# A convolution's LayerNorm, dealt out over the projections beside it: four chunks added on VectorE and one mean product instead of four

## The chip, the core and the metric

The kernel runs on one core of a Trainium2 chip. It is written by hand for the five engines of the core: TensorE (PE, matrix products, with the loading of its weights shown as PEld), VectorE (DVE), ScalarE (ACT), GpSimd (POOL) and SyncE (SP, which here issues the DMAs). The metric is the device time of one execution in microseconds (us). A tile is an area of on-chip memory with 128 partitions; a product of TensorE lands in one of eight PSUM banks.

## The reference, cut to what matters

Two layers of an encoder are computed for 1024 prompt tokens and 32 sample tokens, with a model width of 1024. The change touches layer 0, the convolution branch. Shortened:

```python
h = einsum('btd,de->bte', x, w_in)                     # all projections of the layer
a_val, a_glu, a_gate, q, k, v, b_gate, f_logit = split(h)
a = a_val * sigmoid(a_glu)                             # 512 channels
a, conv_state = causal_dwconv(a, past_conv, conv_w, conv_b)   # 31 taps for each channel
a = silu(layer_norm(a, cln_g, cln_b)) * silu(a_gate)   # LayerNorm over the 512 channels
...                                                    # q, k, v: attention with forgetting, gated by silu(b_gate)
y = einsum('bte,ed->btd', concatenate([a, o]), w_out)
x = layer_norm(ALPHA * x + y, ln_g, ln_b)
```

The channels lie on the partitions, so the 512 channels are four chunks of 128, and the mean over channels is a sum over partitions and chunks. The kernel makes it with TensorE: a 128x128 matrix that holds 1/512 everywhere (`mean_w`) times a chunk gives the chunk's share of the mean, on all partitions at once.

## The kernel before, in words

Layer 0 begins with a run of projections on TensorE. The input x is held transposed and as two parts, a rounded one and its remainder (x0h, x0l), and so is each weight (whi, wlo), so that one projection of 128 columns is, for each of four token groups (256, 256, 256 and 288 tokens), 24 products into one PSUM bank: whi·x0h, wlo·x0h, whi·x0l, eight each. `proj_steps` (L194 to L216) makes them; after each eight products it calls `tick`, which counts down the work put off with `defer(n, fn)` and runs what is due. A weight comes as one DMA of 512 KB (`wraw`, L114), which ScalarE rounds to whi (L107) and VectorE turns into wlo (L108).

Order of the projections: the values and gates of the convolution (eight projections, with v between), then `a_gate` (four, L852 to L859), then `b_gate` (four, L860 and L861), then for each of four head pairs k and q (`qk0`). A group's result leaves its bank by a ScalarE instruction (L857, L320, L810). For k and q ScalarE writes further copies (L267, L268, L280 to L283), and VectorE remainders.

The depthwise convolution is on VectorE alone: for each chunk one multiplication (L868) and 30 multiply-adds over 1086 tokens (L870). It reads the padded inputs (`apad0` to `apad3`) and writes `acc`. After it comes the LayerNorm (L871 to L887), by four token groups (`g`): four products of `mean_w` with the chunks of acc add up to the mean in a bank (L875); VectorE subtracts it from each chunk (L879), ScalarE squares (L881), four more products give the variance (L882), ScalarE takes the root (L883), VectorE the reciprocal (L884) and scales each chunk (L887). Then ScalarE's Silu (L893), the product with `sga` (L896), a split in two parts (L107, L108) and two DMAs to scratch memory (L898, L899). Both loops stand under `tc.high_priority()`: the scheduler, which sets a fixed order for each engine when the kernel is built, puts them as early as it thinks that their inputs are there. Each engine then runs its own list in order.

Which banks a use may take is set by a table of roles: "j" projections, "s" sums and scores, "t" transposes, "o" outputs. BULK gives j six banks (0 to 5), BULK1 three (0 to 2), ATT two (0 and 1), with s on 2 and 3. Before, BULK holds until after the last `b_gate` projection, and ATT from there on, for the first k and q too.

After the first k and q (`stacks = steps(qk0(0))`) the memory of the convolution is released and attention begins: GpSimd makes a bias from `ckb` (a DMA of 512 KB, L916), TensorE the scores (L288, L289), and k and q of the next head pair are mixed in between.

Of the kernel before, what the change touches and what calls it, by code (L numbers as in the profile page):

```python
# [10 lines left out]
FT = mybir.dt.float32  # L11
# [21 lines left out]
def tile_encoder(ctx: ExitStack, tc, A, O):  # L33
# [25 lines left out]
    def ps_s():  # L59
        return bank("s")  # L60
# [127 lines left out]
    def proj_cm(*args):  # L188
        for _ in proj_steps(*args):
            pass  # L190
# [66 lines left out]
    def rows_out(pl, src_cols, n, dst):  # L257
        ps = ps_t()
        for c in range(4):
            pe.transpose(ps[:n, c * 128:(c + 1) * 128], src_cols(c), ident)  # L260
        st = pl.tile([32, 512], FT, name="rst", tag="rst", bufs=1)
        act.activation(st[:n], ps[:n], AF.Copy)
        sp.dma_start(dst, st[:n])
# [53 lines left out]
    def sgate_evac(l, p, pl):  # L317
        def f(g, t0, n, ps):
            sg = pl.tile([128, 288], FT, name="sgc", tag="sgc", bufs=4 - l)
            act.activation(sg[:, :n], ps, AF.Silu)  # L320
            sp.dma_start(sgd[4 * l + g][:, p, :], sg[:, :256])
            if n > 256:
                sp.dma_start(sgS[l][:, p, :], sg[:, 256:288])
        return f
# [19 lines left out]
    def steps(gen):  # L344

        while True:
            try:
                next(gen)
            except StopIteration as stop:
                return stop.value  # L350
# [330 lines left out]
    with tc.tile_pool(name="p1", bufs=1, reuse_waits="tile") as p1:  # L681
# [35 lines left out]
        for c in range(4):  # L717
            pe.transpose(pcc[:, c * 30:(c + 1) * 30], cc[:, c * 128:(c + 1) * 128], ident[:30, :30])
        apad = []
        for c in range(4):  # L720
            ap_ = p1r.tile([128, 1116], FT, name=f"apad{c}")
            pool.memset(ap_[:, 0:30], 0.0)
            act.activation(ap_[:, 1054:1084], pcc[:, c * 30:(c + 1) * 30], AF.Copy)
            apad.append(ap_)
# [127 lines left out]
    for c in range(4):  # L852
        if c == 0:
            defer(60, forget_sums)

        def ev_ag(g, t0, n, ps, c=c):
            act.activation(sga[:, c, t0:t0 + n], ps, AF.Silu)  # L857
        proj_cm(w0, 1024 + c * 128, 128, X0, ev_ag)
    for p in range(4):  # L859
        proj_cm(w0, 3072 + p * 128, 128, X0, sgate_evac(0, p, p1r))  # L860


    rows_out(p1r, lambda c: apad[c][:, 1024:1054], 30, O["conv_p"])
    rows_out(p1r, lambda c: apad[c][:, 1086:1116], 30, O["conv_s"])
    acc = p1r.tile([128, 4, 1086], FT, name="acc")
    for c in range(4):
        ac = acc[:, c]
        dve.tensor_scalar(ac, apad[c][:, 0:1086], vT[:, c, 0:1], vT[:, c, 31:32], op0=OP.mult, op1=OP.add)  # L868
        for j in range(1, 31):
            dve.scalar_tensor_tensor(ac, apad[c][:, j:j + 1086], vT[:, c, j:j + 1], ac, op0=OP.mult, op1=OP.add)  # L870
    with tc.high_priority():  # L871
        for g, (s0, n) in enumerate(((0, 256), (256, 256), (512, 256), (768, 318))):
            pm = ps_s()[:, :n]
            for c in range(4):
                pe.matmul(pm, mean_w, acc[:, c, s0:s0 + n], start=c == 0, stop=c == 3)  # L875
            pvv = ps_s()[:, :n]
            rstd = p1r.tile([128, 318], FT, name="rstd", tag="rstd", bufs=2)
            for c in range(4):
                dve.tensor_tensor(acc[:, c, s0:s0 + n], acc[:, c, s0:s0 + n], pm, op=OP.subtract)  # L879
                sq = p1r.tile([128, 318], FT, name="sq", tag="sq", bufs=2)  # L880
                act.activation(sq[:, :n], acc[:, c, s0:s0 + n], AF.Square)  # L881
                pe.matmul(pvv, mean_w, sq[:, :n], start=c == 0, stop=c == 3)  # L882
            act.activation(rstd[:, :n], pvv, AF.Sqrt, bias=epst)  # L883
            dve.reciprocal(rstd[:, :n], rstd[:, :n])  # L884
            for c in range(4):
                av = acc[:, c, s0:s0 + n]
                dve.tensor_tensor(av, av, rstd[:, :n], op=OP.mult)  # L887
    with tc.high_priority():
        sgh, acl = sga.bitcast(FR), acc.bitcast(FR)
        for g, (s0, n) in enumerate(((0, 256), (256, 256), (512, 256), (768, 318))):  # L890
            for c in range(4):
                av = acc[:, c, s0:s0 + n]
                act.activation(av, av, AF.Silu, bias=vT[:, c, 33:34], scale=vT[:, c, 32:33])  # L893
            for a0, b0, m, dst in ((s0, s0, 256, cad[0][g]), (1054, SEQ, DS, caS[0]))[:1 + g // 3]:
                av = acc[:, :, a0:a0 + m]
                dve.tensor_tensor(av, av, sga[:, :, b0:b0 + m], op=OP.mult)  # L896
                split(sgh[:, :, b0:b0 + m], acl[:, :, a0:a0 + m], av)
                sp.dma_start(dst[0], sga[:, :, b0:b0 + m])  # L898
                sp.dma_start(dst[1], av)  # L899

    got0, got1 = {}, {}

# [4 lines left out]
    def resid1(t, rows, r, c0):  # L907
        sp.dma_start(r[:rows, c0:], x1d[t][:rows, c0:c0 + r.shape[1] - c0])

    roles.update(ATT)  # L910
    stacks = steps(qk0(0))
    cctx.close()
    with tc.tile_pool(name="p2", bufs=1, reuse_waits="tile") as p2:
        def fox_bias(h):
# [694 lines left out]
```

## Time and profile before

| what | value |
| --- | --- |
| median of 3 runs | 1265.44 us (1259.82 to 1269.61) |
| the profiled execution | 1263.32 us, its span 1261.3 us (2.0 us lie around it) |
| PE busy | 1195.5 us, 95% of the span |
| VectorE busy | 984.0 us, 78% |
| ScalarE busy | 709.4 us, 56% |
| mean granted clock of TensorE | 0.990 of full speed |

A busy PE in this profile is one whose pipeline holds a product, so the busy share alone doesn't tell how fast work goes through. The start times of successive rows do: what a group of products costs in the queue is the start of the next group less its own start. The stretch that matters lies between about 216 us (the convolution's last multiply-adds) and about 307 us (the first work of attention).

### The profile page before, as it was taken

The page shows a single profiled execution, that of the slowest core. Times are in us where ns is not written, and L with a number is a line of the kernel's source. Part 1 is how long each engine was busy: PE and PEld are TensorE (multiplying, and loading weights), DVE is VectorE, ACT ScalarE, POOL GpSimd, SP SyncE. Part 2 cuts the span into 40 slices and gives each one's busy share as a digit, 9 for nine tenths or more (in the row PEclk, how much of TensorE's full clock was granted, in tenths as well). Part 3 has the DMA queues.
Part 4 walks back from the last instruction along what each step waited for, and adds up shares of the span by engine and source line. Part 5 has one row for each costly group of instructions (what it writes and reads, how often), then busy time and mean ns, then how long its engine had stood idle before and what let it go on. Part 6 is the DMA issues. An engine that isn't in the chain of part 4 may idle for free.

```text
span 1261.3 us, 25216 instructions
## 1 busy us (share of the span) xinstructions
PE 1195.5 (95%) x9351; PEld 1133.3 (90%) x9353; DVE 984.0 (78%) x2061; ACT 709.4 (56%) x1525; POOL 263.9 (21%) x590
## 2 busy tenths in 40 slices
PE   8999999998998988999999999999899999889997
PEld 7999999998888987999987999999888888869997
DVE  5699999367877778648948979999688878896376
ACT  5111241379787887322257789787577877874110
POOL 0000034002433333000111257666211111100000
PEclk9999999999999999999999999999999999899899
DMA  7113422236332274533252232323333223624412
GB/s 225 51 35 94 124 59 63 80 117 181 86 92 85 68 235 153 186 114 118 84 133 61 82 99 58 93 69 82 82 83 88 61 76 96 203 91 163 122 39 100
DMA packets 163302, 130.29 MB, mean 103 GB/s; under 512 B 35850, under 2 KB 151010, under 8 KB 163180
## 3 DMA queue, kind: packets, MB, share of 16 engines
q1 hardware_dynamic: 163180, 128.69, 34.5%
q8 instruction: 73, 1.20, 0.4%
q14 instruction: 49, 0.40, 0.1%
HBM read 82.93 MB, written 40.31 MB: 98 GB/s over the span
## 4 chain that ended last, share of the span: by engine, by line
PE 66%; DVE 13%; ACT 11%; issue 4%; DMA 3%; SPq 1%; POOL 1%; DVEq 0%; ACTq 0%; POOLq 0%
PE bank L207 31%; PE bank L571 14%; PE bank L240 4%; PE bank L419 3%; PE bank L394 3%; ACT s L373 2%; PE bank L288 2%; PE bank L289 2%; DVE ptl L108 2%; DVE wt L1088 1%; ACT pth L107 1%; DMA rps<-rpx 1%; DVE s L370 1%; PE bank L223 1%; PE bank L252 1%
## 5 line engine op out<-in xcount | busy, mean ns | idle before, releaser
L870 DVE SCALAR_TENSOR_TENSOR acc<-apad,vT,acc 128x1086 f32<-128x1086 f32 x120 | 156.2, 1340 | 1.1
L108 DVE TENSOR_TENSOR ptl<-bank,pth 128x512 fp32r<-128x512 f32 (+1 forms) x160 | 99.3, 633 | 39.2 <-ACT pth L107 37.9
L207 PE MATMUL bank<-x1h,whi 128*128 128x256 f32 (+3 forms) x848 | 125.9, 286 | 0.1
L207 PE MATMUL bank<-x1l,whi 128*128 128x256 f32 (+3 forms) x848 | 124.9, 287 | 0.0
L207 PE MATMUL bank<-x1h,wlo 128*128 128x256 f32 (+3 forms) x848 | 123.8, 286 | 0.0
L207 PE MATMUL bank<-x0h,whi 128*128 128x256 f32 (+1 forms) x768 | 113.7, 288 | 1.5 <-ACT kr L810 1.0
L207 PEld LDWEIGHTS bank<-x1h,whi 128*128 128x128 f32 (+1 forms) x848 | 111.8, 187 | 2.1 <-ACT rpx L979 0.5
L207 PEld LDWEIGHTS bank<-x1h,wlo 128*128 128x128 f32 (+1 forms) x848 | 112.3, 187 | 1.5
L419 PE MATMUL bank<-ident,s 128*128 128x128 f32 x576 | 96.7, 281 | 17.8 <-DVE ptl L108 11.4
L207 PEld LDWEIGHTS bank<-x1l,whi 128*128 128x128 f32 (+1 forms) x848 | 111.9, 188 | 0.9
L207 PE MATMUL bank<-x0h,wlo 128*128 128x256 f32 (+1 forms) x768 | 111.7, 286 | 0.0
L373 ACT ACTIVATE s<-s,mn 128x896 f32<-128x896 f32 (+7 forms) x128 | 98.8, 773 | 22.3 <-DVE mn L370 21.2
L207 PE MATMUL bank<-x0l,whi 128*128 128x256 f32 (+1 forms) x768 | 110.4, 284 | 0.0
L107 ACT ACTIVATE pth<-bank 128x512 fp32r<-128x512 f32 (+1 forms) x160 | 85.8, 549 | 35.8 <-PE bank L419 33.8
L108 DVE TENSOR_TENSOR wlo<-wraw,whi 128x1024 fp32r<-128x1024 f32 (+2 forms) x62 | 75.3, 1215 | 39.2 <-ACT whi L107 39.1
L207 PEld LDWEIGHTS bank<-x0h,whi 128*128 128x128 f32 x768 | 101.4, 190 | 3.7 <-ACT kr L810 1.3
L1112 ACT ACTIVATE jka<-sc,neg 128x768 bf16<-128x768 f32 (+2 forms) x96 | 99.6, 1037 | 4.3 <-POOL neg L1139 1.7
L207 PEld LDWEIGHTS bank<-x0h,wlo 128*128 128x128 f32 x768 | 100.8, 189 | 0.8
L207 PEld LDWEIGHTS bank<-x0l,whi 128*128 128x128 f32 x768 | 100.0, 188 | 0.7
L107 ACT ACTIVATE whi<-wraw 128x1024 fp32r<-128x1024 f32 (+2 forms) x62 | 65.0, 1049 | 57.0 <-PE bank L207 35.5
L419 PEld LDWEIGHTS bank<-ident,s 128*128 128x128 f32 x576 | 67.0, 142 | 32.9 <-DVE ptl L108 11.3
L394 PE MATMUL bank<-pth,v 128*128 128x256 f32 x320 | 92.6, 308 | 3.0 <-ACT pth L107 2.6
(422 smaller groups left out, 2705.0 us busy)
## 6 DMA issues: line engine op xcount, KB each, us to landing
wraw<-in_o_w_in_dram SPq DMA_DIRECT2D x26, 512.0 KB, 4.1
wraw<-in_e_w_in_dram SPq DMA_DIRECT2D x24, 512.0 KB, 4.1
sgd<-sgc SPq DMA_DIRECT2D x32, 128.0 KB, 3.0
out_dram<-ko SPq DMA_DIRECT2D x16, 256.0 KB, 2.3
vf<-vd SPq DMA_DIRECT2D x16, 256.0 KB, 3.3
ckb<-ckd SPq DMA_DIRECT2D x8, 512.0 KB, 4.6
sg<-sgd SPq DMA_DIRECT2D x32, 128.0 KB, 2.7
wraw<-in_e_w_out_dram SPq DMA_DIRECT2D x8, 512.0 KB, 3.9
```

Source lines behind the costliest of these rows:

```text
L107: up = act.activation(hi, src, AF.Copy)
L108: eng.tensor_tensor(lo, src, hi.bitcast(FT), op=OP.subtract)
L207: pe.matmul(ps, w[:, k, :], x[g][:, k, :], start=i == 0, stop=i == 23)
L240: pe.matmul(ps, x[g][:, k, off:off + rows], ws[k // 4][wi][:, k % 4, :], start=i == 0, stop=i == 23)
L288: pe.matmul(ps, qz[:, e, c0:c0 + m], k2[:, k0:k0 + n], start=True, stop=False)
L289: pe.matmul(ps, q2[:, c0:c0 + m], k2[:, k0:k0 + n], start=False, stop=True)
L373: act.activation(s[:, :n], s[:, :n], AF.Exp, bias=mn[:, c:c + 1], scale=-1.0, accum_out=grp[p, i][0][:, j, e:e + 1])
L394: pe.matmul(po[:, j0 * 128:j0 * 128 + w], v2[e][:, k, :], src[:, b0:b0 + w], start=k == 0 and x == 0, stop=k == 2 * i + 1 and x == 1)
L419: pe.transpose(ps[:, c:c + 128], pt[j][:, k * 128:(k + 1) * 128], ident)
L571: pe.matmul(ps, lhs(j, k), ws[k // 4][wi][:, k % 4, :], start=i == 0, stop=i == 23)
L870: dve.scalar_tensor_tensor(ac, apad[c][:, j:j + 1086], vT[:, c, j:j + 1], ac, op0=OP.mult, op1=OP.add)
L1112: act.activation(jka[:, :n], sct[COL[ND + j]], AF.Sign, bias=neg[:, j:j + 1].bitcast(FT), accum_out=cnta[:, j:j + 1]))
```

## The change

The four padded inputs become one tile with four slices. The LayerNorm is written as small functions over a token group and is put off by `defer`, so that its steps fall to fixed steps of the projections: groups 0 and 1 from the start of the third `b_gate` projection on, groups 2 and 3 eighteen steps later, and the last ones within the first k projection. For the mean, VectorE adds the chunks (two additions: chunks 0 and 1 to chunks 2 and 3, then the two results) into the convolution's inputs, which are no longer needed, and one product with `mean_w` makes the mean; for the variance the same is done with the squares. That product is kept in program order on TensorE. Subtraction, squaring and scaling each take all four chunks in one instruction. The roles BULK1 hold from the third `b_gate` projection until the first q is done. The two small outputs of the convolution's state (`rows_out`) move ahead of the third projection.

```diff
+        apads = p1r.tile([128, 4, 1116], FT, name="apads")
         for c in range(4):
-            ap_ = p1r.tile([128, 1116], FT, name=f"apad{c}")
+            ap_ = apads[:, c]
...
+    def convolve():
+        for c in range(4):
+            ac = acc[:, c]
+            dve.tensor_scalar(ac, apad[c][:, 0:1086], vT[:, c, 0:1], vT[:, c, 31:32], op0=OP.mult, op1=OP.add)
+            for j in range(1, 31):
+                dve.scalar_tensor_tensor(ac, apad[c][:, j:j + 1086], vT[:, c, j:j + 1], ac, op0=OP.mult, op1=OP.add)
+        rows_out(p1r, lambda c: apad[c][:, 1024:1054], 30, O["conv_p"])
+        rows_out(p1r, lambda c: apad[c][:, 1086:1116], 30, O["conv_s"])
+
+    def each(x):
+        return x.rearrange("p (o n) -> p o n", o=1).to_broadcast([128, 4, x.shape[1]])
+
+    def add_up(x, s0, n):
+        y = apads[:, :, s0:s0 + n]
+        dve.tensor_tensor(y[:, 0:2], x[:, 0:2], x[:, 2:4], op=OP.add)
+        dve.tensor_tensor(y[:, 0], y[:, 0], y[:, 1], op=OP.add)
+
+    def mean(s0, n):
+        ps = ps_s()[:, :n]
+        tc.keep_in_program_order(pe.matmul(ps, mean_w, apads[:, 0, s0:s0 + n], start=True, stop=True))
+        means[s0] = ps
+
+    def centre(s0, n):
+        av = acc[:, :, s0:s0 + n]
+        dve.tensor_tensor(av, av, each(means[s0]), op=OP.subtract)
+        act.activation(apads[:, :, s0:s0 + n], av, AF.Square)
+        add_up(apads[:, :, s0:s0 + n], s0, n)
+
+    def scale(s0, n):
+        rstd = p1r.tile([128, 318], FT, name="rstd", tag="rstd", bufs=2)
+        act.activation(rstd[:, :n], means[s0], AF.Sqrt, bias=epst)
+        dve.reciprocal(rstd[:, :n], rstd[:, :n])
+        av = acc[:, :, s0:s0 + n]
+        dve.tensor_tensor(av, av, each(rstd[:, :n]), op=OP.mult)
...
+    def conv_plan():
+        for g, (s0, n) in enumerate(((0, 256), (256, 256), (512, 256), (768, 318))):
+            at = 18 * (g // 2) + g % 2
+            for k, fn, *args in ((1, add_up, acc[:, :, s0:s0 + n], s0, n), (3, mean, s0, n), (5, centre, s0, n),
+                                 (10, mean, s0, n), (12, scale, s0, n), (16, curve, s0, n), (18, gate, g, s0)):
+                defer(at + k, fn, *args)
+
     for p in range(4):
+        if p == 2:
+            roles.update(BULK1)
+            convolve()
+            conv_plan()
         proj_cm(w0, 3072 + p * 128, 128, X0, sgate_evac(0, p, p1r))
...
-    with tc.high_priority():
-        for g, (s0, n) in enumerate(((0, 256), (256, 256), (512, 256), (768, 318))):
-            pm = ps_s()[:, :n]
-            for c in range(4):
-                pe.matmul(pm, mean_w, acc[:, c, s0:s0 + n], start=c == 0, stop=c == 3)
-            pvv = ps_s()[:, :n]
...
+    stacks = steps(qk0(0))
+    flush()
     roles.update(ATT)
-    stacks = steps(qk0(0))
```

`curve` and `gate` do what L891 to L899 did (Silu for each chunk, the gate's product, the split, the two DMAs).

Three places show how the engines' lists change. The first is TensorE's list within the third and fourth `b_gate` projections (`bank_...` is a projection's or a sum's bank; x0h and x0l are the input's parts). Before:

```order
L207 MATMUL bank_2664<-x0h_185,whi 128x288 x4
L875 MATMUL bank_2953<-acc,mean_w 128x256 x4
L207 MATMUL bank_2664<-x0h_185,whi 128x288 x4
L207 MATMUL bank_2664<-x0h_185,wlo 128x288 x8
L207 MATMUL bank_2664<-x0l_186,whi 128x288 x8
L207 MATMUL bank_2693<-x0h_179,whi 128x256 x5
L882 MATMUL bank_2958<-sq,mean_w 128x256 x2
L207 MATMUL bank_2693<-x0h_179,whi 128x256 x3
L882 MATMUL bank_2958<-sq,mean_w 128x256 x2
```

After the change, from the start of the third projection:

```order
L260 MATMUL bank_2696<-ident,apads 30x128 x4
L260 MATMUL bank_2704<-ident,apads 30x128 x4
L207 MATMUL bank_2712<-x0h_179,whi 128x256 x8
L207 MATMUL bank_2712<-x0h_179,wlo 128x256 x8
L207 MATMUL bank_2712<-x0l_180,whi 128x256 x8
L884 MATMUL bank_2744<-apads,mean_w 128x256
L207 MATMUL bank_2746<-x0h_181,whi 128x256 x8
L884 MATMUL bank_2755<-apads,mean_w 128x256
```

The first mean stood near the end of the third projection, as four products; now it stands after that projection's first group, as one, and the transposes of the state's output (L260) stand ahead of the projection instead of after the fourth.

The second place is ScalarE's list at the end of the LayerNorm, which now runs beside the first k and q (kr and qr are their copies out of the banks, qz a further copy for q, sga the split of the result). Before:

```order
L893 ACT_TABLE_LOAD
L893 ACTIVATE acc<-acc,vT 128x318 x4
L296 ACTIVATE ko<-bank_3258 128x512
L302 ACTIVATE kr<-bank_3266 32x128
L810 ACTIVATE qr<-bank_3241 128x256
L280 ACTIVATE qz<-qr 64x256
```

With the change:

```order
L811 ACTIVATE kr<-bank_3085 128x256
L903 ACT_TABLE_LOAD
L903 ACTIVATE acc<-acc,vT 128x256 x4
L811 ACTIVATE kr<-bank_3124 128x288
L903 ACTIVATE acc<-acc,vT 128x318 x4
L267 ACTIVATE kA<-kr 64x512
L268 ACTIVATE kB<-kr 64x512
L107 ACTIVATE sga<-acc 128x4x256 x2
L296 ACTIVATE ko<-bank_3195 128x512
L302 ACTIVATE kr<-bank_3203 32x128
L811 ACTIVATE qr<-bank_3168 128x256
L107 ACTIVATE whi<-wraw 128x1024
```

Between the first k projection's third copy and the first copy of q there are now two groups' Silu, two splits and a weight's rounding; before, one group's Silu and a weight's rounding stood there, and no split.

The third place is TensorE's list where attention begins (the number behind "bank" is the PSUM bank; kA and qz are the operands of the scores). Before:

```order
L207 MATMUL bank1_3374<-x0l1_182,whi_3156 128x256 x8
L288 MATMUL bank3_3439<-kA_3110,qz_3324 128x512
L289 MATMUL bank3_3439<-kA_3110,qA_3322 128x512
L207 MATMUL bank0_3445<-x0h0_179,whi_3308 128x256 x8
L288 MATMUL bank2_3454<-kA_3110,qz_3324 128x384
```

With the change:

```order
L207 MATMUL bank2_3311<-x0l1_182,whi_3062 128x256 x8
L288 MATMUL bank3_3376<-kA_3012,qz_3261 128x512
L289 MATMUL bank3_3376<-kA_3012,qA_3259 128x512
L207 MATMUL bank0_3382<-x0h0_179,whi_3245 128x256 x8
L207 MATMUL bank0_3382<-x0h0_179,wlo_3246 128x256 x8
L288 MATMUL bank2_3391<-kA_3012,qz_3261 128x384
```

The last group of q was in bank 1 and is in bank 2 now, the bank that the second score product takes.

## Rows read from the trace of the kernel before

**Rows 1.** Windows: busy us (instructions) of PE, PEld, DVE, ACT, POOL; clock; DMA.

```profile
200.00:220.00 20.00, 20.00 (x168) 20.00 (x167) 19.61 (x16) 3.66 (x8) 2.27 (x5) 1.00 0.24 65
240.00:260.00 20.00, 20.00 (x145) 18.91 (x144) 9.51 (x16) 10.51 (x18) 0.00 (x0) 1.00 0.25 74
260.00:280.00 20.00, 20.00 (x134) 17.73 (x132) 11.16 (x17) 14.98 (x28) 0.00 (x0) 1.00 0.33 99
280.00:300.00 20.00, 16.79 (x124) 15.48 (x123) 16.15 (x27) 19.61 (x35) 0.00 (x0) 1.00 0.56 174
```

**Rows 2.** PE's timeline, first mean: start, us, line, tiles, count.

```profile
242.78 2.00 PE L875 MATMUL bank<-acc,mean_w 128*128 128x256 f32 x8
244.43 0.88 PE L207 MATMUL bank<-x0h,whi 128*128 128x288 f32 x4
245.14 1.20 PE L207 MATMUL bank<-x0h,wlo 128*128 128x288 f32 x8
246.18 1.22 PE L207 MATMUL bank<-x0l,whi 128*128 128x288 f32 x8
```

**Rows 3.** Instructions of L875 and L882: count, ns (least, median, most), first and last start.

```profile
L875 PE MATMUL bank<-acc,mean_w x32: 377/379/484, 242.8 to 273.8; 128*128 128x256 f32 x24, 128*128 128x318 f32 x8
...
L882 PE MATMUL bank<-sq,mean_w x32: 378/380/484, 247.9 to 281.4; 128*128 128x256 f32 x24, 128*128 128x318 f32 x8
```

**Rows 4.** PE's timeline, 283 to 300 us: its waits, in brackets with the releaser.

```profile
286.75 0.66 PE L295 MATMUL bank<-ident,kr 128*128 128x128 f32 x4 [1.74 <-ACT rstd L883]
...
288.45 1.21 PE L207 MATMUL bank<-x0h,whi 128*128 128x256 f32 x8 [1.05 <-ACT kr L810]
...
298.83 1.22 PE L207 MATMUL bank<-x0h,whi 128*128 128x256 f32 x8 [0.37 <-ACT qr L810]
```

**Rows 5.** DVE's timeline: convolution's end, LayerNorm, and one 128x512 operation.

```profile
216.14 11.04 DVE L870 SCALAR_TENSOR_TENSOR acc<-apad,vT,acc 128x1086 f32<-128x1086 f32 x8
...
244.81 1.41 DVE L879 TENSOR_TENSOR acc<-acc,bank 128x256 f32<-128x256 f32 x4 [8.41 <-PE bank L875]
...
253.19 1.43 DVE L887 TENSOR_TENSOR acc<-acc,rstd 128x256 f32<-128x256 f32 x4
...
255.86 1.22 DVE L896 TENSOR_TENSOR acc<-acc,sga 128x1024 f32<-128x1024 f32 x1
...
306.79 0.69 DVE L108 TENSOR_TENSOR v<-vf,v 128x512 fp32r<-128x512 f32 x1 [0.94 <-ACT v L107]
```

**Rows 6.** ACT's timeline: a split, and the LayerNorm's end beside k and q.

```profile
257.11 1.06 ACT L107 ACTIVATE sga<-acc 128x1024 fp32r<-128x1024 f32 x1
...
289.52 0.62 ACT L267 ACTIVATE kA<-kr 64x512 fp32r<-64x512 f32 x1
...
290.81 1.28 ACT L893 ACT_TABLE_LOAD   x1
292.11 2.29 ACT L893 ACTIVATE acc<-acc,vT 128x318 f32<-128x318 f32 x4
...
303.71 0.36 ACT L810 ACTIVATE qr<-bank 128x256 f32<-128x256 f32 x1
```

**Rows 7.** PE's timeline where attention begins: first and second score product.

```profile
301.79 0.40 PE L288 MATMUL bank<-kA,qz 128*128 128x512 f32 x1
...
303.19 0.34 PE L288 MATMUL bank<-kA,qz 128*128 128x384 f32 x1
```

**Rows 8.** SP's queue: issue of a weight, the LayerNorm's last store, the biases.

```profile
294.36 0.39 SPq L114 DMA_DIRECT2D wraw<-in_e_w_in_dram  x1
...
299.88 1.23 SPq L899 DMA_DIRECT2D cas<-acc  x1
...
301.92 1.05 SPq L916 DMA_DIRECT2D ckb<-ckd  x2
```

**Rows 9.** The page's part 6: a weight's DMA, count, KB each, us to landing.

```profile
wraw<-in_e_w_in_dram SPq DMA_DIRECT2D x24, 512.0 KB, 4.1
```

**Rows 10.** POOL's timeline: the first bias of attention.

```profile
306.97 2.49 POOL L919 TENSOR_SCALAR s<-ckb,ncq 128x896 f32<-128x896 f32 x2 [104.58 <-DMA ckb<-ckd]
```

More of the change, by code (lines that the diff above doesn't have):

```diff
@@ L858, in tile_encoder @@
         proj_cm(w0, 1024 + c * 128, 128, X0, ev_ag)
+    acc = p1r.tile([128, 4, 1086], FT, name="acc")
+    sgh, acl = sga.bitcast(FR), acc.bitcast(FR)
+    means = {}
+    def convolve():
[6 more added lines that the diff above has]
+        rows_out(p1r, lambda c: apad[c][:, 1086:1116], 30, O["conv_s"])
@@ new lines, in scale, with curve, gate @@
+    def scale(s0, n):
[4 more added lines that the diff above has]
+        dve.tensor_tensor(av, av, each(rstd[:, :n]), op=OP.mult)
+    def curve(s0, n):
+        for c in range(4):
+            av = acc[:, c, s0:s0 + n]
+            act.activation(av, av, AF.Silu, bias=vT[:, c, 33:34], scale=vT[:, c, 32:33])
+    def gate(g, s0):
+        for a0, b0, m, dst in ((s0, s0, 256, cad[0][g]), (1054, SEQ, DS, caS[0]))[:1 + g // 3]:
+            av = acc[:, :, a0:a0 + m]
+            dve.tensor_tensor(av, av, sga[:, :, b0:b0 + m], op=OP.mult)
+            split(sgh[:, :, b0:b0 + m], acl[:, :, a0:a0 + m], av)
+            sp.dma_start(dst[0], sga[:, :, b0:b0 + m])
+            sp.dma_start(dst[1], av)
@@ L860, in tile_encoder @@
         proj_cm(w0, 3072 + p * 128, 128, X0, sgate_evac(0, p, p1r))
-    rows_out(p1r, lambda c: apad[c][:, 1024:1054], 30, O["conv_p"])
-    rows_out(p1r, lambda c: apad[c][:, 1086:1116], 30, O["conv_s"])
-    acc = p1r.tile([128, 4, 1086], FT, name="acc")
-    for c in range(4):
[L867 to L870, printed above, removed]
@@ L871, in tile_encoder @@
-    with tc.high_priority():
-        for g, (s0, n) in enumerate(((0, 256), (256, 256), (512, 256), (768, 318))):
-            pm = ps_s()[:, :n]
-            for c in range(4):
-                pe.matmul(pm, mean_w, acc[:, c, s0:s0 + n], start=c == 0, stop=c == 3)
-            pvv = ps_s()[:, :n]
[L877 to L899, printed above, removed]
```

## The prediction

> **What bounds the kernel now.** I read the busy times by window first, to see which engine sets the pace where the change works. From 200 to 280 us TensorE never stands still, at a granted clock of 1.00 [rows 1]; the reader is to see that VectorE is busy for only 9.51 and 11.16 of 20 us from 240 on, and ScalarE for 10.51 and 14.98. So until 280 us only what leaves TensorE's queue shortens the time, and additions on VectorE have room. From 280 to 300 us it turns: TensorE 16.79, ScalarE 19.61. The second view is TensorE's timeline, for what the LayerNorm costs in its queue [rows 2, 3] and where it waits [rows 4]; the third the timelines of ScalarE, SP and GpSimd at the hand-over to attention, since the gain counts only if they can take it there [rows 6, 8, 10].
>
> **What leaves TensorE.** The first mean is four products, which the profile shows as eight rows. They start at 242.78, and the next projection's at 244.43 [rows 2]: 1.65 us, 0.206 each. There are 32 rows each of L875 and L882 [rows 3], 64 × 0.206 = 13.2 us. One product in place of four leaves 16 rows, 3.3 us: **9.9 us gone**. That reckoning takes the 318-token products (a quarter of the rows) at the price of the 256-token ones; the medians of 379 and 380 ns against a most of 484 say that this errs low.
>
> Behind such a product the projection starts sluggishly: its next four products of 288 tokens take 0.71 us (244.43 to 245.14), where eight take 1.04 (245.14 to 246.18) [rows 2], so 0.19 us more than half. The products interrupt the projections at 11 places now and at 8 then: **0.6 us**.
>
> The three waits sum to 1.74 + 1.05 + 0.37 = **3.2 us** [rows 4]. The first is a transpose of k that takes bank 5 (role t in ATT), where the last variance lay until ScalarE had taken its root; with BULK1 transposes have banks 6 and 7 and sums 3 to 5. The other two are k and q projections with two banks between them; they get three. I count all three as gone: 9.9 + 0.6 + 3.2 = 13.7 us at the end of the first q. The state's transposes (L260) only move.
>
> **What is added on VectorE.** Per token group and sum, one addition of 128x512 (0.69 us) and one of 128x256, at a quarter of 1.43 or 0.36 to 0.42 [rows 5]: eight times 1.1, 9 us. Subtraction and scaling become one instruction of 128x1024, as L896's 1.22, in place of four that take 1.41 and 1.43 [rows 5], so 1.5 us come back. I cost the sum at nothing: 60 us of window hold 36.8 busy [rows 1]. If that cover failed it would show as a wait of a pinned product, below. The price of a subtraction that reads the mean from PSUM, spread over four chunks, isn't shown; between 0.7 (half the work) and 2.4 us (double) I take 1.22, since four single ones reading PSUM cost what four from SBUF do (1.41, 1.43).
>
> **Are the sums there in time?** The first mean is pinned behind 24 products of the third projection. That projection starts 76 products ahead of 242.78; at 20/168 = 0.119 us each [rows 1], at 233.7. With eight transposes (under 1.3 us, at 0.66 for four larger ones [rows 4]) and 2.9 us, TensorE comes to it at 237.9. The convolution ends at 216.14 + 11.04 = 227.2 [rows 5]; a weight's cut (1.22) and four additions (2.2) make 230.6: 7 us to spare. From mean to variance TensorE has seven times eight products, 6.7 us; subtraction, square (1.06, as a split of 128x1024 [rows 6]) and additions need 3.4. The second pair is tighter, since two gate products and two splits stand ahead of it on VectorE: I get the last sum of squares some 4.8 us after the fourth projection's end, and TensorE at its product at 5.3. Cost zero, with half a microsecond to spare.
>
> **The new wait.** After the change the second score product takes bank 2, which holds q's last group until ScalarE has copied it; before, it was another bank. Count from the fourth `b_gate` projection's end. TensorE: 192 products (22.9 us), transposes (1.4), two sums (1.3), then two score products with eight of the next k (303.19 − 301.79 = 1.40 [rows 7]) and eight more (0.95): 28.0. ScalarE can copy k's third group after 72 products, transposes and sums, at 10.5. From there it has no pause: the tail that takes 13.3 us now (290.81 to 303.71 + 0.36) and, new in it, a second Silu of four chunks (at most 2.29), two copies of k (0.72), kA and kB (1.24), a split and a weight's rounding (2.12) [rows 6], 6.4 in all: 30.1. **TensorE waits 2.1 us.** The rounding needs a weight whose DMA is issued 5.5 us ahead of the LayerNorm's last store now, and behind it then [rows 8]; at 4.1 us to landing [rows 9] it may cost up to 0.5 more. I take 2.2.
>
> ScalarE's path has one table load in this tail, and the row puts it at 1.28 us, with the Silu starting 1.30 after it [rows 6]. The Trainium skill ("ScalarE: Activation LUTs", What ACT_TABLE_LOAD costs) adds a drain of about 1.38 us to the load for every switch; by that the wait would be 3.6 us and the time 1253.2. The row shows no such drain here.
>
> **The sum.** 13.7 − 2.2 = 11.5 us. The profiled execution took 1263.32 us, 2.1 below the median of the runs: 1263.3 − 11.5 = 1251.8, which I forecast as **1252**. Behind the first heads the lists of all engines are those of before, so the gain is carried to the end.
>
> **Rivals.**
> *The second pair's sums come late.* Four VectorE instructions of 1.22 us stand ahead of the squares' additions; if all of them become ready only then, TensorE waits 4.9 − 0.5 = 4.4 us at a pinned product: 1256. For it speaks the slim margin; against it, that VectorE is half idle there. The Trainium skill ("Perfetto Trace Analysis", Optimizing Scalar/DVE Operations) says that where VectorE or ScalarE isn't saturated but causes bubbles elsewhere, instructions should be broken up; this change merges four into one. By that rule this rival would be the likeliest; no row here has the merged form yet.
> *The hand-over gives part of it back.* The biases' DMA is issued at 301.92 behind the LayerNorm's last store, and GpSimd starts 5.05 us later [rows 8, 10]. Then a store of k, a weight and v are issued between the two; if ckb lands a weight's 4.1 us later [rows 9], scores wait on GpSimd: 1256.
> *Slower: the pinned product waits for the convolution.* Now sums are placed where the scheduler expects them to be ready; pinned, the first blocks all projections behind it. It decides once the convolution ends over 7 us late: its steps take 11.04/8 = 1.38 us [rows 5], and 120 of them, each 0.16 us slower from the shared tile, eat up cover and gain; at 0.3 slower it is 36 − 7 − 11.5 = 17 us worse, 1281. Against it: slices of the same length and the same order of chunks.
> *It doesn't reach the end:* attention, with VectorE and ScalarE in its loop, takes up what TensorE gains: 1262.
> *More:* no wait on bank 2 and a freer ScalarE (four table loads fewer, 5 us): 1248.
>
> **Chances.** Forecast 0.50, late sums 0.17, hand-over 0.13, slower 0.06, nothing 0.05, more 0.09. One per cent, about what a measurement can tell from no change, is 12.7 us from the median, at 1252.8, so the forecast itself is cut by that line: of its 0.50 I give 0.30 to faster. Faster 0.41 (with "more" and a little of the late sums), same 0.53, slower 0.06. The range: unknown costs reach from 13.7 + 3 saved (1247) to the two rivals at 1256 with the scatter of the runs, some 5 us to a side: 1246 to 1261.
>
> **What would show it.** Right: L884 with 16 rows of PE, no PE wait at L295 or for kr and qr around the first k and q, a wait of about 2 us at the second score product released by qr, GpSimd's first bias some 12 us earlier, at about 295. Wrong: a PE wait at L884 (sums late), released by VectorE; a PE wait at L288 released by GpSimd's or VectorE's work (hand-over); L870 above 1.38 us.

## The result and the profile after

The changed kernel takes 1251.7 us (median of 4 runs, 1250.92 to 1253.72), beside 1265.61 us for the kernel before on the same chip (4 runs): a ratio of 0.9899, 95% interval 0.9871 to 0.9926. Measured once more among the experiments below it gave 1254.13 us and 0.9925 [0.9903, 0.9946]. So it is about 1% faster, with a quarter of a per cent between the two measurements. The profiled execution has a span of 1248.9 us (before 1261.3).

Runs of one kernel lie 3 to 10 us apart, too much for the steps of this study. So each trace is also read at three moments, counted from the end of the convolution's last multiply-add (before: 216.14 + 11.04 = 227.18, [rows 5]; after: 215.67 + 11.04 = 226.71), which no kernel here changes: the first score product, GpSimd's first bias, and the first statistics of layer 0's residual LayerNorm, near the end of the layer. The last one, on VectorE's timeline before:

```profile
526.52 0.75 DVE L624 BATCH_NORM_STATS2 st<-r 128x6 f32<-128x256 f32 x2
```

and after:

```profile
215.67 11.04 DVE L870 SCALAR_TENSOR_TENSOR acc<-apads,vT,acc 128x1086 f32<-128x1086 f32 x8
...
513.48 0.75 DVE L624 BATCH_NORM_STATS2 st<-r 128x6 f32<-128x256 f32 x2
```

299.34 us from the convolution's end before, 286.77 after: **12.6 us gained in layer 0**. The spans differ by 12.4, the medians by 13.9 in this measurement and by 11.0 in the second, so the rest of the kernel keeps the gain, as closely as that can be told: from this moment to the end of the span the traces of this study take between 732.0 and 738.0 us, so that 12.4 comes so near to 12.6 is in part chance. The same moment in the second measurement of the changed kernel gave 12.1; half a microsecond is what this reading can't tell apart.

Where it comes from, in the windows of the profile after (columns as in [rows 1]):

```profile
240.00:260.00 20.00, 20.00 (x160) 19.69 (x159) 14.95 (x16) 14.49 (x23) 0.00 (x0) 1.00 0.33 105
260.00:280.00 20.00, 20.00 (x163) 19.78 (x162) 17.30 (x18) 17.36 (x28) 0.00 (x0) 1.00 0.39 118
280.00:300.00 20.00, 17.45 (x135) 16.25 (x134) 12.30 (x25) 15.16 (x33) 4.97 (x9) 1.00 0.92 268
```

TensorE is as full as before to 280 us, but works off 160 and 163 instructions where it did 145 and 134. VectorE fills from 9.51 and 11.16 to 14.95 and 17.30. The mean products, by line and then on TensorE's timeline:

```profile
L884 PE MATMUL bank<-apads,mean_w x16: 377/379/432, 236.9 to 265.3; 128*128 128x256 f32 x12, 128*128 128x318 f32 x4
```

```profile
235.96 1.10 PE L207 MATMUL bank<-x0l,whi 128*128 128x256 f32 x8
236.90 0.59 PE L884 MATMUL bank<-apads,mean_w 128*128 128x256 f32 x2
237.14 1.30 PE L207 MATMUL bank<-x0h,whi 128*128 128x256 f32 x8
238.28 0.60 PE L884 MATMUL bank<-apads,mean_w 128*128 128x256 f32 x2
...
265.04 0.70 PE L884 MATMUL bank<-apads,mean_w 128*128 128x318 f32 x2
...
285.26 0.39 PE L288 MATMUL bank<-kA,qz 128*128 128x512 f32 x1
...
286.95 1.11 PE L207 MATMUL bank<-x0h,wlo 128*128 128x256 f32 x8
289.63 0.44 PE L288 MATMUL bank<-kA,qz 128*128 128x384 f32 x1 [1.57 <-ACT qr L811]
...
297.88 0.50 PE L288 MATMUL bank<-kA,qz 128*128 128x512 f32 x1 [0.78 <-DVE mn L370]
```

Sixteen rows in place of 64 [rows 3], none with a wait, and a single product costs 0.24 us (236.90 to 237.14). The eight projections behind it take 1.14 us, where eight undisturbed ones take 0.94. The first score product comes 16.1 us earlier, counted from the convolution. The three waits of [rows 4] are gone. New are the wait at the second score product, for q's copy out of bank 2, and behind it waits for VectorE's reductions (mn), which need GpSimd's biases.

The hand-over to attention, on ScalarE's, SP's and GpSimd's timelines:

```profile
270.39 1.28 ACT L903 ACT_TABLE_LOAD   x1
271.69 2.09 ACT L903 ACTIVATE acc<-acc,vT 128x256 f32<-128x256 f32 x4
...
289.21 0.36 ACT L811 ACTIVATE qr<-bank 128x256 f32<-128x256 f32 x1
```

```profile
284.20 1.31 SPq L911 DMA_DIRECT2D cas<-acc  x1
...
287.20 0.43 SPq L114 DMA_DIRECT2D wraw<-in_e_w_in_dram  x1
287.67 0.67 SPq L448 DMA_DIRECT2D vf<-vd  x1
288.44 1.67 SPq L943 DMA_DIRECT2D ckb<-ckd  x2
```

```profile
295.03 3.05 POOL L946 TENSOR_SCALAR s<-ckb,ncq 128x896 f32<-128x896 f32 x2 [93.11 <-DMA ckb<-ckd]
```

The first bias starts 11.9 us earlier than in [rows 10] (11.5 counted from the convolution), so 4.6 us of TensorE's 16.1 are not matched there.

### The profile page after: what moved, and what is told of

It is laid out like the page before. It is cut to its first block, busy times and chain, and to the rows that moved or that the text cites. A ratio compares the mean times of both kernels' runs of the same rounds, so it can differ in the third digit from the quotient of the medians.

```text
span 1248.9 us, 25084 instructions
## 1 busy us (share of the span) xinstructions
PE 1185.3 (95%) x9303; PEld 1128.0 (90%) x9305; DVE 993.5 (80%) x2053; ACT 702.0 (56%) x1509; POOL 259.6 (21%) x590
## 4 chain that ended last, share of the span: by engine, by line
PE 68%; DVE 13%; ACT 11%; issue 5%; DMA 2%; SPq 1%; POOL 1%; DVEq 0%; ACTq 0%; POOLq 0%
PE bank L207 33%; PE bank L571 15%; PE bank L240 4%; PE bank L419 3%; PE bank L394 3%; PE bank L288 2%; ACT s L373 2%; PE bank L289 2%; ACT pth L107 2%; DVE ptl L108 1%; DVE s L370 1%; PE bank L223 1%; DVE wt L1115 1%; DVE rpx L1015 1%; PE bank L252 1%
## 5 line engine op out<-in xcount | busy, mean ns | idle before, releaser
L870 DVE SCALAR_TENSOR_TENSOR acc<-apads,vT,acc 128x1086 f32<-128x1086 f32 x120 | 156.3, 1342 | 1.1
```

## The experiments

All moments in one table: us by which a kernel is ahead (-) of or behind (+) the kernel before, counted from the convolution's end in each trace, and the ratio of the timed runs to the kernel before.

| kernel | first score | first bias | end of layer 0 | ratio, 95% interval |
| --- | --- | --- | --- | --- |
| changed | -16.1 | -11.5 | -12.6 | 0.9899 [0.9871, 0.9926] |
| changed, again | -16.0 | -11.7 | -12.1 | 0.9925 [0.9903, 0.9946] |
| four products | -5.1 | -3.8 | -4.4 | 0.9972 [0.9956, 0.9988] |
| added, not dealt out | -1.9 | -2.8 | -2.0 | 0.9980 [0.9964, 0.9995] |
| roles alone | -2.5 | +5.8 | +4.6 | 1.0028 [1.0015, 1.0040] |
| changed without roles | -13.7 | -11.4 | -12.6 | 0.9905 [0.9883, 0.9926] |
| changed, other bank | -16.1 | -11.8 | -12.0 | 0.9900 [0.9876, 0.9924] |
| split on VectorE | -16.1 | -13.4 | -12.4 | 0.9905 [0.9878, 0.9933] |
| ckb from GpSimd's queue | -16.1 | -16.9 | -14.9 | 0.9887 [0.9860, 0.9915] |
| ckb and other bank | -16.0 | -16.9 | -14.9 | 0.9881 [0.9861, 0.9902] |
| all three | -16.1 | -18.4 | -10.9 | 0.9902 [0.9871, 0.9932] |
| added twice | -15.8 | -11.0 | -10.6 | 0.9929 [0.9904, 0.9954] |

The last column of moments needs one reservation. From the convolution's end to that moment TensorE's granted clock is 1.00 (2.4 GHz) in the trace before and in six of the twelve in the table; the other six hold a stretch near 0.5 (1.2 GHz): "added, not dealt out" from 277.2 to 290.9 us, within and behind a long wait; "roles alone" from 315.8 to 322.6, among waits of the scores; "other bank" and "added twice" from 301.0 to 304.4, behind waits of 1.42 and 1.97 us; "split on VectorE" and "all three" from about 463 to 467, behind a wait of 0.56 us that other traces have at this place at full clock. What such a stretch costs shows best in the last two. On GpSimd's timeline of "split on VectorE":

```profile
460.31 2.21 POOL L946 TENSOR_SCALAR s<-ckb,ncq 128x256 f32<-128x256 f32 x2 [2.19 <-PE bank L419]
...
473.58 1.48 POOL L946 TENSOR_SCALAR s<-ckb,ncq 128x1024 f32<-128x1024 f32 x2 [10.38 <-ACT pth L107]
```

From the one to the other are 13.27 us, and the same in "all three"; in the changed kernel 11.95 (459.46 to 471.41). So 1.3 us of these two kernels' last moment are the clock's. In "other bank" and "added twice" it is at most 1.1. The changed kernel (both times), four products, the change without roles and the two kernels that only move ckb and the bank (-14.9) can be compared as they stand.

**Four products again.** The changed kernel with

```diff
-        tc.keep_in_program_order(pe.matmul(ps, mean_w, apads[:, 0, s0:s0 + n], start=True, stop=True))
+        for c in range(4):
+            tc.keep_in_program_order(pe.matmul(ps, mean_w, x[:, c, s0:s0 + n], start=c == 0, stop=c == 3))
```

and without `add_up`. 

> The changed kernel with each mean made by four products on TensorE again, at the same steps and in program order, and without the additions on VectorE. Theory (the gain is what left TensorE's queue): 48 more product rows at 0.206 us each, 9.9 us, all of them ahead of the last root, so everything behind is as much later; VectorE's missing additions bring at most 1 us back at the last variance. 1261 us, a ratio of about 0.996 to the kernel before. Rival (the dealing out and the new order bring the gain, not the number of products): within 1 us of the changed kernel's 1251.7, a ratio of 0.989.

1259.95 us, 0.9972. TensorE waits at none of the products:

```profile
L885 PE MATMUL bank<-acc,mean_w x32: 377/378/431, 237.6 to 266.4; 128*128 128x256 f32 x24, 128*128 128x318 f32 x8
...
L885 PE MATMUL bank<-apads,mean_w x32: 378/379/431, 247.8 to 277.0; 128*128 128x256 f32 x24, 128*128 128x318 f32 x8
```

The 48 further rows bring the first score 16.06 - 5.11 = 11.0 us later, 0.228 us a row, and the layer's end 8.2 us. The theory's size holds and the rival falls: two thirds of the gain at the layer's end are the products that left TensorE.

**Added, but not dealt out.** The kernel before with `add_up`, `mean`, `centre` and `scale` of the change, under `tc.high_priority()` at the old place, without BULK1:

```diff
+    with tc.high_priority():
+        for s0, n in ((0, 256), (256, 256), (512, 256), (768, 318)):
+            add_up(acc[:, :, s0:s0 + n], s0, n)
+            mean(s0, n)
+            centre(s0, n)
+            mean(s0, n)
+            scale(s0, n)
```

> The kernel before with the additions on VectorE, one product for each mean and the merged subtraction and scaling, but with the LayerNorm where it was: placed by the scheduler's own reckoning, not dealt out over the steps, its last variance behind the first k, and without BULK1. TensorE's queue has the same 16 products as in the changed kernel. Theory (the time follows GpSimd's first bias, which stands behind the last variance, ScalarE's tail and the last stores): the last variance comes some 5 us earlier than before, at 276, the first bias about as much, at 301 to 303: 1259.5, ratio 0.995 to 0.997. Rival (all of the gain is what left TensorE's queue, wherever it stands): 1253, ratio 0.990 to 0.992.

1262.51 us, 0.9980: both were too fast, and the theory's mechanism isn't what holds it. TensorE stands still at the last variance, behind the first k:

```profile
272.52 1.21 PE L207 MATMUL bank<-x0l,whi 128*128 128x288 f32 x8
280.81 1.40 PE L884 MATMUL bank<-apads,mean_w 128*128 128x318 f32 x2 [7.08 <-DVE apads L880]
```

It waits for VectorE, whose timeline shows why the addition is late:

```profile
274.59 2.36 DVE L915 TENSOR_TENSOR acc<-acc,sga 128x1024 f32<-128x1024 f32 x2
276.94 1.23 DVE L108 TENSOR_TENSOR acc<-acc,sga 128x1024 fp32r<-128x1024 f32 x1
278.10 0.82 DVE L879 TENSOR_TENSOR apads<-apads 128x636 f32<-128x636 f32 x1
279.04 1.23 DVE L108 TENSOR_TENSOR acc<-acc,sga 128x1024 fp32r<-128x1024 f32 x1
280.19 0.48 DVE L880 TENSOR_TENSOR apads<-apads 128x318 f32<-128x318 f32 x1
```

The sums stand behind the gates and splits of earlier groups, in instructions of 1.2 us. The products left TensorE here too, and 7 of the 11 us come back as one wait. The wait costs more than its length: during it the granted clock falls to 0.51 and stays there from 277.2 to 290.9 us, and the projections behind it take 1.87 us for eight products (284.91 to 286.78) instead of 0.95:

```profile
284.91 2.07 PE L207 MATMUL bank<-x0h,whi 128*128 128x256 f32 x8 [0.96 <-ACT kr L811]
286.78 1.91 PE L207 MATMUL bank<-x0h,wlo 128*128 128x256 f32 x8
```

Against the same products of the changed kernel, the rows from 284.91 to 291.02 lose some 2.7 us to the clock (an estimate). The change without the roles, below, has the same additions dealt out and no such wait; so the additions are free only where their place in VectorE's list is early enough.

**The roles alone.** The kernel before with

```diff
-    roles.update(ATT)
+    roles.update(BULK1)
     stacks = steps(qk0(0))
+    roles.update(ATT)
```

> The kernel before with the roles BULK1 in place of ATT for the first k and q, and nothing else: the LayerNorm stays where it was, up to the first k. Theory (terms add up): the three waits of 1.74, 1.05 and 0.37 us go, 3.2 us at the end of the first q; but here the hand-over is bound by ScalarE and SP, which gain nothing, so at most 3 and more likely 1 us reaches the end: 1262.5 to 1264.5 against 1265.6 before, ratio 0.997 to 0.999. Rival (the banks are the gain): 1252 to 1256, ratio 0.990 to 0.993. Rival (bank 2 of the second score product costs as much as the waits that go): no difference, ratio 1.000.

1268.05 us, slower: none of the three expected that. TensorE gains the 2.5 us at the first score product, as it should; but SP's queue is ordered anew:

```profile
302.06 1.32 SPq L114 DMA_DIRECT2D wraw<-in_e_w_in_dram  x2
303.48 1.31 SPq L448 DMA_DIRECT2D vf<-vd  x1
304.92 1.96 SPq L917 DMA_DIRECT2D ckb<-ckd  x2
```

```profile
312.61 2.10 POOL L920 TENSOR_SCALAR s<-ckb,ncq 128x896 f32<-128x896 f32 x2 [110.34 <-DMA ckb<-ckd]
```

Two weights stand right ahead of ckb, where in [rows 8] the weight was issued 7.6 us before it. It is issued 3.0 us later and takes 7.7 us to the first bias instead of 5.05. The first bias is 5.8 us behind, the layer's end 4.6: TensorE ahead, biases behind, and the biases decide (the stretch at half clock lies behind the late bias and adds to the loss, by how much was not measured). From here on that was the theory.

**The changed kernel without the roles** (`roles.update(BULK1)` left out, ATT from the first k on). 

> The changed kernel without BULK1 ahead of attention: BULK through the third and fourth b_gate projections, ATT from the first k on, as in the kernel before. Theory: the wait of 1.57 us at the second score product goes; in its place TensorE waits some 1 us for kr and 0.4 us for qr within k and q, where two banks are left, and the hand-over (scores wait for the biases of GpSimd) is as late as in the changed kernel: within 1.5 us of 1251.7, ratio 0.988 to 0.991. Rival (the roles carry a quarter of the gain): 1255, ratio 0.9915 or more.

1251.99 us, 0.9905, and the same end of layer 0. In place of the wait on bank 2 TensorE waits within q:

```profile
281.49 1.21 PE L207 MATMUL bank<-x0h,whi 128*128 128x256 f32 x8 [0.81 <-ACT qr L811]
...
285.33 1.22 PE L207 MATMUL bank<-x0h,whi 128*128 128x256 f32 x8 [0.73 <-ACT qr L811]
```

The roles bring the first score product 2.4 us forward and the end nothing.

**Another bank for q's last group** (`turn["j"] += 1` behind `roles.update(BULK1)`). 

> The changed kernel with the turn of the projections' banks moved on by one, so that q's last group lies in bank 0 and the second score product takes a bank that is free. Theory (the next thing that TensorE waits for, the reduction over the bias that GpSimd makes once ckb has landed at 294, is not moved): the wait of 1.57 us at the second score product goes, the third score product's waits grow by the same, and the time stays within 0.6 us of 1251.7, ratio 0.9885 to 0.9895. Rival (the wait on the bank is itself the loss): 1.6 us faster, 1250.1, ratio 0.9877.

1251.01 us, 0.9900; the wait on qr goes and the next score product's grows from 0.78 to 1.42:

```profile
299.51 0.50 PE L288 MATMUL bank<-kA,qz 128*128 128x512 f32 x1 [1.42 <-DVE mn L370]
```

The layer's end (-12.0) is no earlier than in the changed kernel, though the half clock here may hide up to 1.1 us. The two kernels with ckb moved, below, settle it at full clock: with the wait and without it the layer ends at -14.9. The wait that the prediction charged costs nothing at the layer's end: what is behind it waits for the biases anyway.

**The last groups' split on VectorE** (`split(..., alone=g > 1)` in `gate`). 

> The changed kernel with the split of the last two token groups' result made by VectorE alone (its rounding copies in place of ScalarE's, 2.0 + 0.3 us of ScalarE's tail behind the second Silu). Theory (after the change the hand-over to attention is bound by ScalarE's tail, the stores behind it and the landing of ckb): q's last copy comes some 2 us earlier, the wait of 1.57 us at the second score product goes, GpSimd's first bias comes 1 to 1.5 us earlier than 295.0, and the time falls by about as much: 1250.3, ratio 0.988. Rival (TensorE's queue alone sets the end): no difference, 1251.7, ratio 0.989.

1252.21 us, 0.9905: no difference that the runs can tell, and the wait stays (1.85 us). The table's first bias comes 1.7 to 1.9 us earlier, but ScalarE's copies of q are no faster: there is one buffer for qr, and ScalarE now waits for VectorE to be done with it, whose queue the two copies lengthened:

```profile
285.00 0.41 ACT L811 ACTIVATE qr<-bank 128x288 f32<-128x288 f32 x1 [1.73 <-DVE qB L285]
```

The -12.4 at the layer's end doesn't speak against the biases, for the half clock took 1.3 us of it: at GpSimd's bias at 460.31, just ahead of that stretch, this kernel is 1.2 us ahead of the changed one (1.6 of its second trace). So nearly all of the earlier bias was kept as long as the clock was the same.

**ckb from GpSimd's queue.**

```diff
-            sp.dma_start(ckb, bass.AP(...))
+            (pool if h < 2 else sp).dma_start(ckb, bass.AP(...))
```

> The changed kernel with the biases' first two DMAs (ckb of heads 0 and 1) issued from GpSimd's queue, which is idle there, in place of SP's, where they stand behind the LayerNorm's last stores, ko, kr, a weight and v. Theory (the time follows GpSimd's first bias: against the kernel before it came 11.9 us earlier in the changed kernel, 3.5 earlier with four products, 5.6 later with the roles alone, and the times moved by 13, 3.5 and minus 3.5): the first bias starts at 275 to 290 in place of 295; the TensorE waits released by VectorE's reductions (0.78, 0.17, 0.20) go, the wait for qr stays: 1 to 3 us faster, 1249.7, ratio 0.9875. Rival (TensorE or ScalarE is the bound of attention's beginning whatever ckb does): no difference, 1251.7, ratio 0.989.

1249.67 us, 0.9887. GpSimd's timeline:

```profile
266.06 0.77 POOL L943 DMA_DIRECT2D ckb<-ckd  x1 [64.14 <-PE bank L884]
289.05 0.54 POOL L943 DMA_DIRECT2D ckb<-ckd  x1 [22.21 <-DMA out_dram<-kr]
289.62 2.11 POOL L947 TENSOR_SCALAR s<-ckb,ncq 128x896 f32<-128x896 f32 x2
```

Head 0's biases are fetched as soon as the last mean product has freed the memory, 22 us sooner; the first bias then waits only behind the issue for head 1. The waits for mn at the first scores are gone, the wait for qr (1.57) is still there, and the layer ends 2.3 to 2.7 us earlier than in the changed kernel. That is some five times what the moment scatters; the timed ratio alone doesn't separate it.

**ckb and the other bank together.** 

> The changed kernel with two edits at the hand-over: the first two ckb issued from GpSimd's queue, and the projections' banks moved on by one. Theory (attention's beginning is held first by the biases, and behind them by the bank that waits for qr): the biases come 5 us earlier than in the changed kernel, as with the first edit alone, and TensorE no longer waits 1.57 us at the second score product; the end of layer 0 comes 2.3 us earlier by the first edit and 0 to 1.5 by the second: 1248.5, ratio 0.9865 to 0.9885. Rival (the second edit costs what it cost alone, 0.6 us at the end of layer 0): 1250, ratio 0.989.

1249.31 us, 0.9881; the changed kernel measured beside it has 1254.13 us and 0.9925, and each of the six runs here (1246.11 to 1250.83) is faster than each of the six there (1250.95 to 1256.19). The end of layer 0 is that of the first edit alone: the second brings nothing here. This version beats both kernels, by 1.2% the kernel before.

**All three edits.** 

> The changed kernel with three edits on the hand-over at once: the projections' banks moved on by one, the last two groups' split on VectorE, the first two ckb from GpSimd's queue. Theory: the 1.57 us wait on the bank and the waits for VectorE's reductions (1.15 us) go, and little else stands still there: 2 to 4 us faster than the changed kernel, 1248.7, ratio 0.9865. Rival (attention takes the gain up, ScalarE's exponentials are as late): 1251.7, ratio 0.989.

1250.8 us, 0.9902. The first bias is the earliest of all (-18.4), and layer 0 ends 4 us later than without the split on VectorE. TensorE waits at the third score product:

```profile
293.29 0.50 PE L288 MATMUL bank<-kA,qz 128*128 128x512 f32 x1 [2.36 <-DVE mn L370]
```

That is 1.0 more than with two edits (1.32). Counted from the convolution's end, this kernel is 1.5 us ahead of the one with two edits at the first bias, 0.7 behind at the bias at 327.00, and 2.7 behind at the next, at 335.99: the two are 9.0 us apart here and 7.0 there. The half clock at 463 takes the last 1.3 of the 4 us. Why the lists of this kernel lose the 2.7 was not followed. They show the theory's limit: an earlier first bias alone does not bring an earlier end.

**Every addition made twice.**

```diff
         dve.tensor_tensor(y[:, 0:2], x[:, 0:2], x[:, 2:4], op=OP.add)
+        dve.tensor_tensor(y[:, 2:4], x[:, 0:2], x[:, 2:4], op=OP.add)
         dve.tensor_tensor(y[:, 0], y[:, 0], y[:, 1], op=OP.add)
+        dve.tensor_tensor(y[:, 1], y[:, 0], y[:, 1], op=OP.add)
```

> The changed kernel with every addition of the LayerNorm made twice on VectorE (the second result goes to a slice that nobody reads), some 9 us more work there. Theory (additions cost nothing as long as a sum is there when TensorE comes to its product; the last pair's sums of squares had 0.3 us to spare, the others several us): no wait at the first pair's products, 1 to 2.5 us at the last variances, 1253.3, ratio 0.9905. Rival (VectorE has room for all of it): no difference, 1251.7, ratio 0.989. Rival (VectorE's work is on the path): 9 us slower, 1260.7, ratio 0.996.

1254.05 us, 0.9929. The size is the theory's (the layer's end 1.5 to 2.0 us later), the way isn't: TensorE doesn't wait at the products, because the scheduler put the last two of them two and ten products further back. The bias comes half a microsecond later, the third score product waits 1.97 for mn, and up to 1.1 us of the rest is the half clock behind that wait. Some 9 us more on VectorE cost 2 or less, so the 9 us that the change added are not on the path.

**The changed kernel again.** 

> The changed kernel once more, unchanged, beside the other two, to tell how far its time and the moments read from its trace scatter. All theories: ratio 0.988 to 0.991, and the end of layer 0 (first statistics of the residual LayerNorm) within 0.3 us of the first time, 12.7 us ahead of the kernel before.

 0.9925, above the range, and 12.1 us at the layer's end, 0.5 below the first time: that is the scatter used above.

## Why the prediction was right, and where its terms were off

The forecast of 1252 us was met, by two terms that were both too small and in part cancelled. That it was met to 0.3 us is luck: it counts from the profiled execution, 2.1 us below the median of the kernel before, and the second measurement of the changed kernel gave 1254.13. The gain to hold against its 11.5 is the one at the layer's end, 12.6 and 12.1.

- **Products leaving TensorE: 9.9 us predicted, 11.0 measured** for the same 48 rows. The price from [rows 2] (0.206) fits the 64 rows of the kernel before: 13.2 us by the starts of the rows, as predicted. It was wrong for the 16 that stay, 3.3 us predicted: a single product costs less than two rows of a series, 0.24 to 0.30 rather than 0.41, and all eight together 2.1.
- **Sluggish restarts:** 0.19 us a place was right (1.14 for eight projections against 0.94 to 0.95).
- **The three waits:** all gone, as predicted; the roles alone and the change without them put their worth at the first score product at 2.5 and 2.4 us, against 3.2. With the products this makes 13.4 of the 16.1 us there; the restarts are 0.6 of the rest, and 2 us, with the new order of the sums, no single run isolates. By the rows of the two traces, where the waits are the 3.2 of [rows 4], some 1.8 us are left for the projections' slower starts behind products and behind waits, where the prediction has 0.6.
- **The sums are in time:** right, and as narrow as said. The first group's sum ends at 229.72 at the latest, and TensorE comes to its product at 236.90, the 7 us predicted; the last sum of squares ends at 264.22 + 0.49 = 264.71, TensorE comes at 265.04, 0.3 us later, where 0.5 was predicted. On VectorE's timeline:

```profile
228.97 0.75 DVE L880 TENSOR_TENSOR apads<-apads 128x256 f32<-128x256 f32 x2
...
238.92 1.22 DVE L889 TENSOR_TENSOR acc<-acc,bank 128x1024 f32<-128x1024 f32 x1 [0.16 <-PE bank L884]
...
264.22 0.49 DVE L880 TENSOR_TENSOR apads<-apads 128x318 f32<-128x318 f32 x1
```

  The subtraction that reads the mean from PSUM takes the 1.22 us assumed. The rival of late sums did not come, but its mechanism is real: without the dealing out it is the 7.08 us above. The Trainium skill ("Perfetto Trace Analysis", Optimizing Scalar/DVE Operations) advises breaking up instructions that hold up another engine; the rows of that experiment show such instructions of 1.2 us ahead of the sum, but the change removed the wait by the place of the sums, not by their size.
- **The new wait of 2.2 us: the step that failed.** The wait is there, 1.57 us, released by qr as said. But it isn't what the gain is paid back with: taken away, it changed nothing. Of 16.1 us at the first score product 12.6 arrive at the layer's end, so 3.5 us are lost, and they are lost at the hand-over, the rival with a chance of 0.13: ckb stands behind the last stores, ko, kr, a weight and v, and GpSimd starts at 295.03 (the prediction said about 295). ckb is issued 3.2 us behind the first score product (285.26 and 288.44), where before it was 0.1 (301.79 and 301.92), and the bias starts 6.6 us behind its issue instead of 5.05: together the 4.6 us that the first bias lost on TensorE. The prediction had GpSimd's new start right, and put the waiting for it among the rivals instead of into the sum. The sign that the prediction gave for it stands in the trace too, the wait for mn at 297.88. With ckb out of that queue 2.3 to 2.7 of the 3.5 us came back; where the last 1 us goes no run shows.
- **The table load** takes 1.28 us and the Silu starts 1.30 after it, as in [rows 6]; the drain of the Trainium skill ("ScalarE: Activation LUTs", What ACT_TABLE_LOAD costs) shows here no more than there.
- **Carried to the end:** 12.6 us at layer 0's end, 12.4 in the span, 13.9 and 11.0 in the medians: right, within the scatter.
- The slower rival (a convolution behind the product) is out: eight steps take 11.04 us as before.

Net: 16.1 - 3.5 = 12.6 us where the prediction had 13.7 - 2.2 = 11.5.

## What to carry to other kernels

Read a gain on the full engine twice: where it is made, and behind the next hand-over, from a moment that no variant moves; the difference is what the hand-over keeps, and the wait that shows there first need not be the one that costs. Work moved to an engine with room is free only if its place in that engine's list is early enough: the same additions cost 7 us of waiting, and by estimate 2.7 us more at half clock, where the scheduler placed them, and nothing where they were dealt out over fixed steps. Look at the granted clock of a stretch before comparing moments behind it: two traces here seemed to speak against the biases by 1.3 us that were the clock's. When a stage starts on a DMA, look at what stands ahead of it in its queue, since moving anything else may put a weight there.

## What was not expected of the hardware

VectorE and GpSimd held each other up, in all three kernels that move ckb. With the biases early, they meet the rounding of a weight; VectorE's and GpSimd's timelines of the kernel with ckb and the other bank:

```profile
289.71 3.39 DVE L108 TENSOR_TENSOR wlo<-wraw,whi 128x1024 fp32r<-128x1024 f32 x1 [1.53 <-ACT whi L107]
```

```profile
289.91 2.11 POOL L948 TENSOR_SCALAR s<-ckb,ncq 128x896 f32<-128x896 f32 x2
291.98 1.70 POOL L950 TENSOR_SCALAR_AFFINE_SELECT s<-s 128x128 f32<-128x128 f32 x2
...
294.70 0.53 POOL L950 TENSOR_SCALAR_AFFINE_SELECT s<-s 128x128 f32<-128x128 f32 x2
```

The rounding, alone 1.23 us, takes 2.16 more, about the 2.11 of GpSimd's two biases; the selects behind them take 1.70 instead of 0.53, 1.17 more, about the rounding's own time. The Trainium skill ("SBUF — State Buffer", SBUF: two separate sides) says that a VectorE instruction with two inputs from SBUF and a GpSimd instruction that reads SBUF lock a shared pair of ports for a whole instruction each; these rows agree with that. Which of the two goes first can't be told from the rows: VectorE's starts 0.2 us before GpSimd's here and is the one held up.

A DMA landed the later the more was issued just ahead of it: from the issue of ckb to the first bias 5.05 us with v ahead (kernel before; 5.9 in "added, not dealt out"), 6.6 with a weight and v (changed; 6.2 to 6.8 in the six other traces with that order), 7.7 with two weights and v (roles alone). No run changes this alone.
